# A decoder layer on one core: the low parts of every second weight chunk in three quarters of the MLP by an accumulating DMA

## The chip, the cores and the metric

The kernel runs on one core of one Trainium2 chip. The metric is the time of the whole program on the device, in microseconds, the median over runs. A profiled execution gives, beside that, a trace of every engine: TensorE (PE, its weight loads PEld), VectorE (DVE), ScalarE (ACT), GpSimd (POOL), SyncE (SP, which issues the loads) and the 16 DMA engines.

## What is computed

One layer of a hybrid decoder for 256 tokens of width 2048: three token mixers on one input projection (sliding-window attention, gated delta rule, cross-attention over memory tokens), a gated merge, an output projection, an MLP of width 8192, and a last norm, all with fp32 weights.

```python
n = rms_norm(h, g_mix[l])
p = n @ w_in[l]
...
merged = g_a * (y_a @ w_swa_up[l]) + g_b * (y_b @ w_gdn_up[l]) + g_c * (y_c @ w_xa_up[l])
h = h + merged @ w_out[l]
u = rms_norm(h, g_mlp[l]) @ w_mlp_in[l]
h = h + jnp.square(jax.nn.relu(u)) @ w_mlp_out[l]
...
return rms_norm(h, g_final)
```

The change is in the last three quarters of the two MLP products.

## The kernel before

**Products in high and low parts.** Every weight and activation is held as the sum of two numbers of type `float32r`: a high part (the fp32 value rounded) and a low part (what rounding left). A product is made of high by high, high by low and low by high.

**The weight stream.** All weights come as a stream of 496 chunks, in the order of use. A chunk is 128 partitions by 1024 fp32, 512 KB: two blocks of 128 rows of the weights by 512 columns. A chunk is loaded from SP's queue into a buffer `raw` (`issue_dma`; 4 buffers, `RAW`), ACT copies it into `whi`, which rounds it, and DVE makes `wlo = raw - whi` (`split`, L234 to L237; 4 buffers each, `SPL`). `weights` (L143) is called by a strip for each chunk. It first issues loads up to AHEAD + RAW - 1 = 5 chunks ahead and splits up to AHEAD = 2 chunks ahead, in program order. A buffer is free for its next chunk when the last reader of the chunk before is done: for `raw` that is DVE's subtraction, for `whi` and `wlo` the last matmul.

**Strips.** `strip_w` (L157) computes 512 output columns with the weights as the stationary operand: per chunk 8 pairs of matmuls, L168 with 512 moving columns (high and low activations at once) and L169 with 256. `strip_x` (L182, through `mm_x`) keeps activations stationary and moves weights: per chunk 12 matmuls of 512 columns, three for each of two blocks of rows and two halves of the tokens (L178 to L180). Both kinds of strip have 8 chunks.

**The MLP** (L160 on) goes by quarters of the hidden width: in each, 4 strips of the first kind make the hidden values, and 4 of the second kind add their part to the output. The hidden values are moved out of PSUM by a chain over the engines (`hid_evac`): ACT copies a half (L230), DVE adds (L232) and scales (L1173), POOL squares (L1175), ACT rounds and DVE subtracts (L235, L237 on `ys`). Between the first and the second quarter (`q == 1`) the space of the merged mixers' tile `mg` is given up, and the gain of the last norm, `gf`, is loaded there. Chunks 304 to 495 belong to the last three quarters.

**Order.** Every engine takes its instructions in the order in which the program was written; generators (`start`, `advance`, `run`) lay the steps of a split or of a chain a hop at a time beside the products.

Of the kernel before, what the change touches and what calls it, by code (L numbers as in the profile page):

```python
# [10 lines left out]
F32 = mybir.dt.float32  # L11
# [12 lines left out]
CW = 1024  # columns per partition of a chunk of streamed weights  # L24
# [3 lines left out]
TAIL = 3         # last chunks that stay on chip together  # L28
# columns in which the output is scaled and stored: whether by the scalar engine, which
FIN = (0, slice(0, 256)), (1, slice(1536, 2048)), (0, slice(256, 1536))  # L30
# The background work is a row of steps, taken at a rate per tick (a block of products of the main stream), so
# that what a step reads has been made by then: rates of attention and decays, of the delta rule, of the
# convolution, of the sliding window.
RATE_A, RATE_B, RATE_C, RATE_S = 0.53, 0.5, 0.6, 0.83
# ticks between a sum in PSUM and what follows it, in the output projection; before its norm
OUT, WO = 8, 3
# chunks at which x's squares, its scaling and the norm of the memory tokens begin
XSQ, XSC, MRS = 4, 13, 13
NEG = -1.0e30
RAW, SPL = 4, 4  # chunks loaded, chunks split into high and low parts  # L40
AHEAD = 2        # chunks split ahead of the one in the products

# columns of the packed vectors
V_GMIX, V_GMEM, V_GMLP, V_CONV, V_NORM, V_SINK, V_ALOG, V_DTB, V_END = (
    0, 16, 32, 48, 96, 97, 113, 117, 121)
# blocks of the packed constants
C_ID, C_PREV, C_CUR, C_CUM, C_BLK, C_DEC, C_DECN, C_BS, C_PLACE, C_LVL = range(10)
BS = 16          # block of the lower matrices inverted by substitution
# [5 lines left out]
def tile_layer(ctx: ExitStack, tc: tile.TileContext, xT, memT, wmk, wmv, wq, wkv, wqc, wqkv, wz, wg, wua, wub, wuc, wo, w1, w2, vec, cst, x, gfin, out):  # L54
# [7 lines left out]
    wspl = pool("wspl", SPL)  # L62
# [60 lines left out]
    def pieces(i, w):  # L123
        """The first chunk comes in a block of rows at a time."""
        n = KC if i == 0 else 1
        return [slice(w // n * k, w // n * (k + 1)) for k in range(n)]

    def issue_split(i):
        raw = raws.pop(i)
        w = raw.shape[-1]  # L130
        hi = wspl.tile([P, WMAX], F32R, name="whi")[:, :w]
        lo = wspl.tile([P, WMAX], F32R, name="wlo")[:, :w]
        parts[i] = hi, lo
        fs = before_split[i]
        if i:
            for f in fs:
                f()
        for n, c in enumerate(pieces(i, w)):
            if i == 0:
                fs[n]()  # L140
            start(split(hi[:, c], lo[:, c], raw[:, c]))

    def weights(ncols):  # L143
        """High and low parts of the next chunk of the stream; loads and splits run ahead."""
        i = done[2]
        while done[0] < min(len(stream), i + AHEAD + RAW):
            issue_dma(done[0])
            done[0] += 1
        while done[1] < min(len(stream), i + AHEAD + 1):
# [7 lines left out]
    def strip_w(k0, nk, acts, evac, nblk=4):  # L157
        """out.T = W.T @ acts for 512 columns of W: 128 of them at a time in one PSUM bank, whose
        halves hold the products with the high and with the low parts of acts."""
# [15 lines left out]
    def mm_x(bank, acts, k, tt, hi, lo, first, last):  # L175
        """out (tokens on partitions) += acts.T @ W for one block of 128 rows of W."""
# [5 lines left out]
    def strip_x(acts, evac):  # L182
        """out = acts.T @ W for 512 columns of W, tokens on partitions."""
# [11 lines left out]
    def last_strip_x(acts, evac):  # L195
        """The same in halves of the columns. The last chunks stay on chip together, and the halves of the
        tokens and columns are finished one after the other."""
# [17 lines left out]
    # What engines do to a finished bank, or in the background, is a generator that yields where one  # L215
    # engine hands over to another; tick() moves all of them on by a hop.
# [21 lines left out]

    def split_scaled(hi, lo, src, g):
# [9 lines left out]
    def rsqrt(out, in_, mul, n):  # L249
        """out = (in_ * mul + EPS) ** -0.5 on [P, n]"""  # L250
# [4 lines left out]
    def token_rstd(sums, rows, cols):  # L255
        """From sums of squares per partition and token: 1/rms as a row on each partition, and as a
        column with tokens on partitions."""
# [19 lines left out]
    class Lane:  # L277
        """Generators in a row, each with its rate in hops a tick; one may yield how many hops its last step
        counts for."""
# [39 lines left out]
    def pipelined(tasks, every):  # L319
        """Each task's hops one after the other, with those of the next task beginning `every` hops later."""  # L320
# [27 lines left out]
    # ================= start: memory tokens and x =================  # L348
# [94 lines left out]
    # ================= input projection =================  # L443
# [6 lines left out]
    # the keys of the sliding window, transposed: by kv head the high parts on all rows; the low parts on its rows  # L450
    kp = sw.tile([P, 3, T], F32R, name="kp")
    head_rows = slice(0, 64), slice(64, 128)
    # v of the kv heads by block of keys: [high | low] of the first, [low | high] of the second
# [126 lines left out]
    def decays():  # L580
        dtb = vc_[:, V_DTB:V_DTB + 4].unsqueeze(1).broadcast_to([P, NT, 4])
        # softplus(t) = max(t, 0) + log1p(e), e = exp(-|t|); log1p(e) = ln(w) + (e - (w - 1)) / w, w = 1 + e
# [89 lines left out]
    def delta():  # L672
# [11 lines left out]
        # of a chunk, the columns for w and those for q: [w | q] in the first chunk, [q | w] in the second  # L684
# [591 lines left out]
```

## Time and profile before

| | us |
|---|---|
| median of 3 runs | 1503.67 |
| lowest and highest run | 1499.26, 1503.81 |
| span of the profiled execution, first to last instruction | 1498.2 |
| TensorE busy | 1466.9 (98%) |
| DVE busy | 956.9 (64%) |
| ACT busy | 748.5 (50%) |
| POOL busy | 189.7 (13%) |
| packets of the load queue, share of 16 engines | 54.0% |

The time of a run holds the span and what lies around it; the profiled execution has no time of its own beside the three runs, which are 1.1 to 5.6 us above its span. Busy is the time in which an engine worked on any instruction. Matmuls are pipelined and their ends are modelled, so a busy TensorE isn't one at its peak: how fast it goes is read from the starts of neighbouring matmuls. A mean over the span mixes stages, so what holds in the MLP is read from stretches of it.

### The profile page before, as it was taken

To read this page: it belongs to the slowest core of one execution; us is meant where nothing else is said; L and a number is where in the kernel's file an instruction comes from. 1 tells how busy PE (TensorE), PEld (TensorE's weight loads), DVE (VectorE), ACT (ScalarE), POOL (GpSimd) and SP (SyncE) were. 2 spreads that over 40 slices of the span, in tenths; PEclk is the share of its full clock that TensorE was granted. 3 is DMA by queue.
4 is the path that set the end of the run, shared out by engine and by line. 5 is a ranking of instruction groups with operands and counts; after the bars stand their busy time and mean duration, and the time that the engine had idled before them with its cause. 6 is when DMAs were issued, how large, how long until landed. Compare 5 with 4: busy or idle time off the path is not lost.

```text
span 1498.2 us, 20793 instructions
## 1 busy us (share of the span) xinstructions
PE 1466.9 (98%) x7890; PEld 1251.1 (84%) x7890; DVE 956.9 (64%) x1324; ACT 748.5 (50%) x1115; POOL 189.7 (13%) x244
## 2 busy tenths in 40 slices
PE   6999999998999999999999999999999999999997
PEld 5798888887888888888888888888888888888887
DVE  8866785774667786666557664476455665467554
ACT  5555754553465665454555443355334453345443
POOL 5200032143112210000001000011000010001011
PEclk9999999999999999999999999999999999999999
DMA  7555554444434555556655655655655655555653
GB/s 255 187 171 183 169 175 149 141 167 140 143 118 150 169 167 191 191 170 225 217 176 175 214 185 186 223 183 170 209 185 168 210 185 188 190 189 166 208 191 119
DMA packets 76069, 269.60 MB, mean 180 GB/s; under 512 B 8512, under 2 KB 9152, under 8 KB 75840
## 3 DMA queue, kind: packets, MB, share of 16 engines
q1 hardware_dynamic: 75968, 268.27, 54.0%
q8 instruction: 62, 1.02, 0.3%
q14 instruction: 39, 0.32, 0.1%
HBM read 266.14 MB, written 2.10 MB: 179 GB/s over the span
## 4 chain that ended last, share of the span: by engine, by line
PE 74%; ACT 1%; DVE 1%; issue 0%; DVEq 0%; POOLq 0%; POOL 0%; ACTq 0%
PE mm L168 28%; PE mm L169 14%; PE mm L180 10%; PE mm L179 10%; PE mm L178 10%; PE mm L337 1%; PE mm L954 1%; PE mm L953 0%; ACT whi L235 0%; DVE wlo L237 0%; ACT L975 0%; ACT L1051 0%; PE mm L1006 0%; ACT sg L1051 0%; PE mm L1005 0%
## 5 line engine op out<-in xcount | busy, mean ns | idle before, releaser
L237 DVE TENSOR_TENSOR wlo<-raw,whi 128x1024 fp32r<-128x1024 f32 (+2 forms) x497 | 613.5, 1249 | 349.1 <-ACT whi L235 348.4
L168 PE MATMUL mm<-xs,whi 128*128 128x512 f32 x2240 | 796.6, 397 | 0.4 <-DVE half L232 0.4
L235 ACT CAST whi<-raw 128x1024 fp32r<-128x1024 f32 (+2 forms) x497 | 511.5, 1041 | 434.2 <-PE mm L180 209.1
L169 PE MATMUL mm<-xs,wlo 128*128 128x256 f32 x2240 | 627.5, 280 | 1.1 <-DVE wlo L237 1.1
L168 PEld LDWEIGHTS mm<-xs,whi 128*128 128x128 f32 x2240 | 421.0, 188 | 99.6 <-issue 0.9
L169 PEld LDWEIGHTS mm<-xs,wlo 128*128 128x128 f32 x2240 | 421.4, 188 | 2.6 <-DVE wlo L237 2.0
L180 PE MATMUL mm<-whi,ys 128*128 128x512 f32 (+1 forms) x544 | 209.6, 385 | 0.0
L179 PE MATMUL mm<-wlo,ys 128*128 128x512 f32 (+1 forms) x544 | 207.4, 381 | 0.0
L178 PE MATMUL mm<-whi,ys 128*128 128x512 f32 (+1 forms) x544 | 206.3, 379 | 0.0
L230 ACT COPY half<-mm 128x256 f32<-128x256 f32 x192 | 70.5, 373 | 141.7 <-PE mm L169 140.2
L179 PEld LDWEIGHTS mm<-wlo,ys 128*128 128x128 f32 x544 | 102.1, 188 | 23.3
L178 PEld LDWEIGHTS mm<-whi,ys 128*128 128x128 f32 x544 | 102.1, 188 | 21.5
L180 PEld LDWEIGHTS mm<-whi,ys 128*128 128x128 f32 x544 | 102.3, 188 | 20.7
L1175 POOL TENSOR_TENSOR half<-half 128x256 f32<-128x256 f32 x64 | 40.0, 626 | 577.9 <-DVE half L1173 571.5
L168 PE MATMUL mm<-ys,whi 128*128 128x512 f32 x256 | 91.2, 397 | 0.0
L232 DVE TENSOR_TENSOR half<-mm,half 128x256 f32<-128x256 f32 x120 | 49.2, 418 | 43.7 <-ACT half L230 43.4
L169 PE MATMUL mm<-ys,wlo 128*128 128x256 f32 x256 | 71.8, 280 | 0.0
L1106 DVE TENSOR_TENSOR res<-mm,res 128x512 f32<-128x512 f32 (+1 forms) x42 | 28.0, 666 | 52.3 <-PE mm L180 52.3
L168 PEld LDWEIGHTS mm<-ys,whi 128*128 128x128 f32 x256 | 48.1, 188 | 10.7 <-issue 0.2
L178 PE MATMUL mm<-whi,mg 128*128 128x512 f32 x128 | 50.5, 394 | 0.0
L180 PE MATMUL mm<-whi,mg 128*128 128x512 f32 x128 | 49.9, 390 | 0.0
L179 PE MATMUL mm<-wlo,mg 128*128 128x512 f32 x128 | 49.9, 390 | 0.0
(259 smaller groups left out, 1128.8 us busy)
## 6 DMA issues: line engine op xcount, KB each, us to landing
raw<-in_w SPq DMA_DIRECT2D x256, 512.0 KB, 4.2
raw<-in_wg SPq DMA_DIRECT2D x96, 512.0 KB, 3.3
raw<-in_wo SPq DMA_DIRECT2D x32, 512.0 KB, 4.4
raw<-in_wqkv SPq DMA_DIRECT2D x24, 512.0 KB, 4.0
raw<-in_wq SPq DMA_DIRECT2D x16, 512.0 KB, 3.9
raw<-in_wua SPq DMA_DIRECT2D x16, 512.0 KB, 4.8
raw<-in_wmv SPq DMA_DIRECT2D x8, 512.0 KB, 3.8
raw<-in_wqc SPq DMA_DIRECT2D x8, 512.0 KB, 3.9
```

Source lines behind the costliest of these rows:

```text
L168: nc.tensor.matmul(banks[b], lhsT=hi[:, i, cols], rhs=acts[:, k], start=(k == k0), stop=False)
L169: nc.tensor.matmul(banks[b][:, :T], lhsT=lo[:, i, cols], rhs=acts[:, k, 0], start=False, stop=(last and i == KC - 1))
L178: nc.tensor.matmul(bank, lhsT=acts[:, k, 0, tok], rhs=hi, start=first, stop=False)
L179: nc.tensor.matmul(bank, lhsT=acts[:, k, 0, tok], rhs=lo, start=False, stop=False)
L180: nc.tensor.matmul(bank, lhsT=acts[:, k, 1, tok], rhs=hi, start=False, stop=last)
L230: nc.scalar.copy(out=t, in_=bank[:, T:])
L232: nc.vector.tensor_tensor(out=out, in0=bank[:, :T], in1=t, op=ALU.add)
L235: nc.scalar.copy(out=hi, in_=src)
L237: nc.vector.tensor_tensor(out=lo, in0=src, in1=hi.bitcast(F32), op=ALU.subtract)
L337: nc.tensor.transpose(ps[:, i * P:(i + 1) * P], src_fn(i), ident)
L1106: nc.vector.tensor_tensor(out=v, in0=bank, in1=v, op=ALU.add)
L1175: nc.gpsimd.tensor_tensor(out=t, in0=t, in1=t, op=ALU.mult)
```

## The change

From the second quarter of the MLP on, new chunks are split into a second pool with 6 buffers each of `whi` and `wlo`, which lies where `mg` was, and loads and splits run two chunks further ahead (`AHEAD_2` = 4). Of these chunks those with an odd number are split in another way: ACT copies `raw` into `whi` as before, makes `wlo = -whi` in a second pass, and a DMA issued from POOL then adds `raw` to `wlo` in place. All three are issued at once, without hops between them. Even chunks are split as before. Comments that the change also takes out are left out here.

```diff
-RAW, SPL = 4, 4  # chunks loaded, chunks split into high and low parts
-AHEAD = 2        # chunks split ahead of the one in the products
...
+RAW, SPL = 4, 4
+AHEAD = 2
+AHEAD_2, SPL_2 = 4, 6
...
-    wspl = pool("wspl", SPL)
+    spl = [pool("wspl", SPL)]
...
-        hi = wspl.tile([P, WMAX], F32R, name="whi")[:, :w]
-        lo = wspl.tile([P, WMAX], F32R, name="wlo")[:, :w]
+        late = len(spl) > 1
+        hi = spl[-1].tile([P, WMAX], F32R, name="whi")[:, :w]
+        lo = spl[-1].tile([P, WMAX], F32R, name="wlo")[:, :w]
         parts[i] = hi, lo
+        if late and i % 2:
+            start(split_dma(hi, lo, raw))
+            return
...
-        while done[0] < min(len(stream), i + AHEAD + RAW):
+        ahead = AHEAD if len(spl) == 1 else AHEAD_2
+        while done[0] < min(len(stream), i + ahead + RAW):
             issue_dma(done[0])
             done[0] += 1
-        while done[1] < min(len(stream), i + AHEAD + 1):
+        while done[1] < min(len(stream), i + ahead + 1):
...
+    def split_dma(hi, lo, src):
+
+        nc.scalar.copy(out=hi, in_=src)
+        nc.scalar.activation(out=lo, in_=hi.bitcast(F32), func=AF.Copy, scale=-1.0)
+        nc.gpsimd.dma_start(out=lo, in_=src, accum_op=ALU.add)
+        yield
...
+            spl.append(ctx.enter_context(tc.tile_pool(name="wspl2", bufs=SPL_2)))
```

On ACT, at the end of the first strip of the second quarter, before (L230 copies a sum out of PSUM, `ys` are hidden values, `whi` the copies of chunks; the semaphores that a row waits for stand in brackets, DMAHW for a load, DMASW for a DMA of POOL):

```order
L235 CAST whi<-raw 128x1024 [waits DMAHW7_49,DVE_49,PE_49]
L230 COPY half<-mm 128x256 [waits PE_49] x3
L230 COPY half<-mm 128x256 [waits DVE_49,PE_49]
L235 CAST ys<-half 128x256 [waits Pool_49]
L235 CAST whi<-raw 128x1024 [waits DMAHW0_49]
L235 CAST ys<-half 128x256 [waits Pool_49] x3
L235 CAST whi<-raw 128x1024 [waits DMAHW1_49]
```

And now, at the same place:

```order
L241 CAST whi<-raw 128x1024 [waits DMAHW0_49,DVE_49,PE_49]
L247 CAST whi<-raw 128x1024 [waits DMAHW1_49,PE_49]
L248 ACTIVATE wlo<-whi 128x1024 [waits DMASW1_49,PE_49,Activation_49]
L236 COPY half<-mm 128x256 [waits PE_49] x3
L236 COPY half<-mm 128x256 [waits DVE_49,PE_49]
L241 CAST ys<-half 128x256 [waits Pool_49]
L241 CAST whi<-raw 128x1024 [waits DMAHW2_49]
L241 CAST ys<-half 128x256 [waits Pool_49] x3
L247 CAST whi<-raw 128x1024 [waits DMAHW3_49]
L248 ACTIVATE wlo<-whi 128x1024 [waits DMASW2_49,Activation_49]
```

Ahead of the sums two more chunks have been split, every second chunk takes two passes on ACT, and the second of them waits for the accumulate that filled the same buffer six chunks before.

On SP, the loads of the same strip, before:

```order
L121 DMA raw<-in_w 128x1024 [waits DMAHW3_49,DVE_49]
L121 DMA raw<-in_w 128x1024 [waits DMAHW4_49,DVE_49]
L121 DMA raw<-in_w 128x1024 [waits DMAHW5_49,DVE_49]
L121 DMA raw<-in_w 128x1024 [waits DMAHW6_49,DMAHW2_49,DVE_49]
L121 DMA raw<-in_w 128x1024 [waits DMAHW7_49,DVE_49]
```

And now:

```order
L122 DMA raw<-in_w 128x1024 [waits DMAHW3_49,DMASW1_49]
L122 DMA raw<-in_w 128x1024 [waits DMAHW6_49,DVE_49]
L122 DMA raw<-in_w 128x1024 [waits DMAHW5_49,DMAHW2_49,DMASW2_49]
L122 DMA raw<-in_w 128x1024 [waits DMAHW0_49,DVE_49]
L122 DMA raw<-in_w 128x1024 [waits DMAHW7_49,DMASW3_49]
L122 DMA raw<-in_w 128x1024 [waits DMAHW1_49,DMASW4_49,Activation_49]
L122 DMA raw<-in_w 128x1024 [waits DMAHW2_49,DVE_49]
```

Each load waited for a subtraction on DVE; now, but for one place in eight chunks, every second one waits for an accumulate. TensorE's matmuls stand in the same order as before.

## Rows read from the trace of the kernel before

**Rows 1.** The page: busy us, share of the span, instructions.

```profile
PE 1466.9 (98%) x7890; PEld 1251.1 (84%) x7890; DVE 956.9 (64%) x1324; ACT 748.5 (50%) x1115; POOL 189.7 (13%) x244
```

**Rows 2.** Stretches of the MLP: strips of the first kind, then of the second.

```profile
core 0: us, PE busy (x) PEld busy (x) DVE busy (x) ACT busy (x) POOL busy (x), PEclk, DMA share, GB/s
950.00:1040.00 90.00, 90.00 (x513) 78.29 (x512) 56.21 (x70) 41.17 (x57) 7.50 (x12) 1.00 0.58 194
1040.00:1130.00 90.00, 90.00 (x390) 72.54 (x389) 48.11 (x50) 36.91 (x41) 2.50 (x4) 1.00 0.58 188
```

**Rows 3.** TensorE by line, 940 to 1480: busy us, mean ns, idle us before.

```profile
L168 PE MATMUL mm<-xs,whi 128*128 128x512 f32 x768 | 269.1, 393 | 0.0
...
L178 PE MATMUL mm<-whi,ys 128*128 128x512 f32 (+1 forms) x405 | 154.9, 382 | 0.0
```

**Rows 4.** Waits, 950 to 1480: us in total, times, longest us.

```profile
POOL half L1175 <- DVE half L1173: 502.6, 36, 108.3
DVE wlo L237 <- ACT whi L235: 166.1, 117, 1.7
ACT whi L235 <- PE mm L180: 133.4, 77, 1.8
ACT whi L235 <- PE mm L168: 94.1, 54, 1.8
```

**Rows 5.** The load queue's waits, 950 to 1480.

```profile
SPq L121 <- DVE wlo L237: 360.8, 174, 6.8
```

**Rows 6.** Matmuls in order of time (start us, us), three places.

```profile
719.67 0.39 PE L178 MATMUL mm<-whi,mg 128*128 128x512 f32 x1
...
720.35 0.39 PE L178 MATMUL mm<-whi,mg 128*128 128x512 f32 x1
...
1085.05 0.39 PE L178 MATMUL mm<-whi,ys 128*128 128x512 f32 x1
...
1085.75 0.39 PE L178 MATMUL mm<-whi,ys 128*128 128x512 f32 x1
...
1139.68 0.39 PE L168 MATMUL mm<-xs,whi 128*128 128x512 f32 x1
...
1140.38 0.39 PE L168 MATMUL mm<-xs,whi 128*128 128x512 f32 x1
```

**Rows 7.** DVE by line, 950 to 1480.

```profile
L237 DVE TENSOR_TENSOR wlo<-raw,whi 128x1024 fp32r<-128x1024 f32 x189 | 233.5, 1252 | 166.1 <-ACT whi L235 166.1
```

**Rows 8.** Tile raw, 950 to 1480: ns min/median/max; landing of loads.

```profile
L235 ACT CAST whi<-raw x190: 1031/1048/1058, 949.4 to 1479.0; 128x1024 fp32r<-128x1024 f32 x190
...
L121 SPq DMA_DIRECT2D raw<-in_w x186: 327/328/328, 954.0 to 1472.6; - x186
...
DMA to landing us min/median/max: 3.1/4.2/7.4
```

**Rows 9.** ACT by line and shape, whole span.

```profile
L1051 ACT ACTIVATE sg<-sg 128x1024 f32<-128x1024 f32 x12 | 12.7, 1062 | 0.1
```

**Rows 10.** POOL by line, 950 to 1480.

```profile
L1193 POOL TENSOR_TENSOR res<-res,gf 128x512 f32<-128x512 f32 x6 | 7.8, 1299 | 59.1 <-ACT mm L1110 58.8
```

**Rows 11.** ACT in order of time at a strip's end.

```profile
1019.44 0.37 ACT L230 COPY half<-mm 128x256 f32<-128x256 f32 x1 [0.33 <-PE mm L169]
...
1022.59 0.41 ACT L235 CAST ys<-half 128x256 fp32r<-128x256 f32 x1 [0.68 <-POOL half L1175]
```

**Rows 12.** Stretches at the start, columns as in the second group.

```profile
8.00:12.00 4.00, 3.56 (x10) 2.74 (x11) 3.58 (x3) 3.44 (x7) 3.39 (x2) 1.00 1.01 355
12.00:16.00 4.00, 3.64 (x20) 2.91 (x19) 4.00 (x4) 3.49 (x7) 3.73 (x3) 1.00 1.03 392
16.00:20.00 4.00, 1.41 (x7) 1.05 (x6) 4.00 (x3) 3.65 (x6) 3.84 (x3) 0.92 0.36 139
20.00:24.00 4.00, 4.00 (x16) 3.12 (x14) 4.00 (x3) 0.30 (x1) 3.83 (x3) 0.66 0.91 300
...
32.00:36.00 4.00, 4.00 (x25) 3.55 (x24) 4.00 (x6) 1.05 (x1) 0.00 (x0) 1.00 1.00 381
```

## The prediction

> **What bounds the kernel now.** I read the page's table of busy time first, then a table of stretches for the MLP, then what each engine waits for there, and last the starts of single matmuls. The busy table [rows 1] puts TensorE at 98% of the span, DVE at 64%, ACT at 50%. A mean over stages can mislead, so the stretch table [rows 2] cuts out the part that the change touches, from 950 us on: TensorE is busy 90.00 of 90.00 us in strips of both kinds, at a granted clock of 1.00 (the 2.4 GHz level), while DVE has 56 or 48 us of work, ACT 41 or 37, POOL 7.5 or 2.5 and the DMA engines a share of 0.58. The groups of TensorE in this part [rows 3] show idle time 0.0 in front of all five lines of matmuls (the first and the last of them stand there): nothing that DVE, ACT or a transfer does is late there. The waits [rows 4] run the other way: ACT's copy of a chunk waits for a matmul (the buffer is free only when TensorE is done with it), DVE waits for that copy, and the load queue waits for DVE's subtraction [rows 5]. Feeders wait for TensorE, not TensorE for feeders.
>
> The time of a chunk comes from starts [rows 6]: in a strip with tokens on the output, three matmuls take 1085.05 to 1085.75, 0.70 us, and a chunk has twelve: 2.80 us. In a strip of the first kind, two pairs take 1139.68 to 1140.38, 0.70 us, and a chunk has eight pairs: 2.80 us again. The three quarters have 192 chunks, 538 us. The first two of them are split before the new buffers exist, so of the odd ones 95 are changed.
>
> **What is removed.** 95 subtractions of 1.25 us [rows 7] leave DVE: 119 us of work, all of it in a stretch where TensorE never waited for DVE. Worth nothing on the path: with DVE faster, TensorE is still the next late thing. A chunk's low part was made in time before, and earlier is no use.
>
> **What is added on ACT.** One more pass over 128x1024 per changed chunk. The copy of that shape takes 1.05 us [rows 8], an activation of that shape 1.06 [rows 9], so 95 x 1.06 = 101 us. In 90 us stand 32 chunks, 16 changed, 17 us more on 41 [rows 2]: 58 of 90. ACT stays under two thirds, and its own waits for matmuls (133 + 94 us, [rows 4]) shrink by that much. Cost nothing, covered by those waits.
>
> **What is added on POOL.** 95 issues. POOL sits idle 503 us there for DVE's input to its squares [rows 4]. An issue waits for ACT's second pass, and behind it in POOL's queue stand the squares of a strip's end; but ACT does that pass ahead of the copies that feed those squares (order of ACT above), so the squares are not held longer than the issue itself takes. I bound an issue between the 0.33 us that the load queue spends on one [rows 8] and the 1.3 us of POOL's longest operation there [rows 10], and take 1; it lies beside TensorE's work.
>
> **Is a low part ready in time?** Before, a chunk was split two ahead; now a set of buffers comes back six chunks later, so ACT may begin a chunk when TensorE begins the one five before it: a lead of 5 x 2.80 = 14.0 us. It has to hold 1.05 + 1.06 = 2.1 us on ACT and the accumulate, from the issue to its last byte. No row shows an accumulate. Its nearest row is a load of the same 512 KB, 3.1 us at least, 4.2 in the median, 7.4 at most [rows 8]. Below lies 3.1 (no dearer than a load), above twice the median plus the issue, 9.4; I take 4.2 and a second pass over the bytes, 1.4 (next part): 5.6. Then 2.1 + 5.6 = 7.7 of 14.0, and 6.3 us are over; even 9.4 fits. At the end of a strip of the first kind ACT first moves out the sums: from the last copy at 1019.44 to the last cast at 1022.59 + 0.41 it is held 3.6 us [rows 11]. The next odd chunk then has 10.4 us for its 7.7.
>
> **Do the raw buffers come back in time?** This is the added wait: the load queue, one row for all loads, now waits in every second row for an accumulate instead of a subtraction (order of SP above), and every later load stands behind it. The slot that an accumulated chunk leaves goes to the chunk five later (one time in four: four later), a subtracted chunk's to the third or fourth after it. Over eight chunks a slot passes one of each: 2.1 + 5.6 + a load of 4.2, and 1.05 + 1.25 + 4.2, together 18.4 of the 22.4 us that eight chunks last. The one return after four chunks (11.9 us against 11.2) is 0.7 late, and the 6.3 us of lead cover it. TensorE waits only if accumulate plus two loads exceed 18 us (now 14.0). Cost nothing; without that cover it would be 24 times the excess.
>
> **Do the DMA engines keep up?** This is the term that decides. In three stretches at the start they are all busy (share 1.00 to 1.03) and move 381 and 392 GB/s, once 355 [rows 12]. At 386, 524,288 bytes take 1.36 us of all engines. Two chunks last 5.60 us; their loads need 2.72, so an accumulate may cost **2.88 us** before the transfers bound. Below: one pass, 1.36 (then 4.08 of 5.60). Above: three passes in turn, raw read, low part read, low part written, 4.08 (then 6.80). I take two passes, 2.72, since in a load reading and writing already run side by side and count once, and the add has one read more. That is 5.44 of 5.60, 97%: the transfers fit, with almost no room. The Trainium skill ("Collectives: The Full Stack", The bandwidth ceiling) says of adds in the transfer path that two source reads slow them, not the add; by it the cost is two passes and the sum stays 0, and no run here shows it.
>
> **Sum.** 0 on DVE, ACT, POOL, lead, slots and DMA engines. The last chunk is odd too, but its low part is due 7.7 us after a start 14.0 us ahead, and TensorE's end is as before. So the profiled execution would again span 1498.2 us. The runs lie 1.1 to 5.6 us above that span, their median 5.5; forecast at the median, **1503.7**.
>
> **Rivals.** First, *slower: the DMA engines become the bound.* The place is the load queue in the last three quarters, the point 2.88 us per accumulate. Beyond it each pair of chunks lasts longer by the excess: 95 x (cost - 2.88), less the 6 us of lead. At 3.2 us: 30 - 6 = +24, 1528. At 4.08: 114 - 6 = +108, 1612. Against it: only a third pass or a transfer slower than a load reaches it. For it: 97% leaves 0.16 us, and a single slow engine of sixteen holds up the whole transfer. A fall of the granted clock is not added: it fell to 0.66 after a stretch in which TensorE was busy 1.41 of 4.00 us [rows 12], and here it would be busy over 80%. The Trainium skill ("DMA: Bandwidth & Descriptors", Latency and other measured facts) says that engines 7 and 15 are usually slower, by a guess because of transfers issued from POOL; no trace here has such a transfer, and 3% would be enough.
>
> Second, *slower: the raw buffers come back late,* if accumulate plus two loads exceed 18 us, say 9 + 2 x 5 = 19: 24 times 1.0, less 6: +18, 1522. Loads of 7.4 us occur [rows 8], but as the longest of 186.
>
> Third, *faster: a shorter matmul pitch.* Three matmuls on the tile `mg` take 719.67 to 720.35, 0.68 us [rows 6], against 0.70 on `ys`, though shapes and moving buffers are the same. So operands, by place or by value, can move the pitch by 3%. The new buffers lie where `mg` lay. If the 96 chunks of the second kind of strip took 4 x 0.68 = 2.72 us, that is 96 x 0.08 = -7.7, 1496. Against it: no row tells place from value, and `ys` and its values stay. It might as well go up by as much, 1511.
>
> That the change does nothing is not a rival but the forecast: DVE's 119 us go, and the time does not.
>
> **How the numbers follow.** About 0.3% (4.5 us) is what a measurement of this kernel can tell from no change. Forecast, within it: 0.54. DMA engines: of costs between 1.36 and 4.08, those beyond 2.88 + (6 + 4.5)/95 = 2.99 are 40%; I give 0.30, since two passes are the likeliest. Late slots 0.06. Pitch: 0.08 down, 0.02 up. So faster 0.08, same 0.54, slower 0.38. The range goes from 1495 (pitch gain) to 1558, an accumulate of (54 + 6)/95 + 2.88 = 3.5 us; that leaves out about half of the DMA case and little else.
>
> **What would show it.** Right: subtractions of this size on DVE down by 95, DVE near 840 us, ACT near 850, TensorE's idle time in the last three quarters still 0.0, a DMA share up to 0.97 or less, accumulates landing 4 to 8 us after issue. The DMA rival: share near 1.0 there, TensorE waiting for an accumulate or ACT's copy waiting for a load. The slot rival: the same waits at a share well below 1. Pitch: three matmuls off 0.70 us without idle time. The forecast is wrong if an accumulate costs more than 2.99 us of the sixteen engines or needs more than 10 us to land.

## The result, and the profile after

The changed kernel takes 1547.33 us (median of 4, 1545.97 to 1551.86) where the kernel before takes 1501.56 on the same chip: a ratio of 1.0308, 95% interval 1.0291 to 1.0324. It is 46 us slower. The time lies in the range given, but the forecast was no change; the direction was wrong. The profiled execution spans 1544.2 us against 1498.2, so 46.0 us are to be found in it.

Busy time over the whole span, columns as in [rows 1]:

```profile
PE 1478.2 (96%) x7890; PEld 1250.7 (81%) x7890; DVE 844.6 (55%) x1229; ACT 844.4 (55%) x1210; POOL 271.6 (18%) x339
```

DVE fell by 112 us and ACT rose by 96, as intended, and it bought nothing. The same two stretches as in [rows 2]:

```profile
950.00:1040.00 90.00, 85.38 (x479) 73.30 (x478) 37.14 (x54) 52.50 (x68) 20.77 (x27) 1.00 0.96 259
1040.00:1130.00 90.00, 85.14 (x370) 67.25 (x369) 26.62 (x33) 48.91 (x53) 15.53 (x19) 1.00 0.96 257
```

TensorE, full before, is busy 85 of 90 us in both kinds of strip, at the same granted clock of 1.00; it has 479 matmuls in the first stretch where [rows 2] has 513. The DMA engines' share went from 0.58 to 0.96. TensorE by line, 940 to 1480 us, answering to [rows 3] (L174 and L175 are the strips of the first kind, L184 to L186 those of the second):

```profile
L174 PE MATMUL mm<-xs,whi 128*128 128x512 f32 x768 | 271.2, 395 | 0.0
L175 PE MATMUL mm<-xs,wlo 128*128 128x256 f32 x768 | 216.6, 282 | 15.9 <-DMA wlo<-raw 15.6
L185 PE MATMUL mm<-wlo,ys 128*128 128x512 f32 x332 | 133.5, 402 | 12.7 <-DMA wlo<-raw 12.6
L184 PE MATMUL mm<-whi,ys 128*128 128x512 f32 x333 | 131.3, 394 | 0.0
```

The two lines that read low parts now wait, nearly always for the accumulating DMA; over the whole span the page has 17.0 and 19.4 us for them, and the rest of the 46 stands in TensorE's busy time (1478.2 against 1466.9), probably because a matmul that is held within a group is drawn longer. That names who waits last, not why. The waits of the feeders, 950 to 1480, answer to [rows 4], and those of the load queue to [rows 5]:

```profile
ACT whi L247 <- DMA raw<-in_w: 124.3, 62, 7.7
...
ACT whi L241 <- DMA raw<-in_w: 74.6, 46, 3.5
...
ACT whi L241 <- PE mm L186: 2.6, 1, 2.6
```
```profile
SPq L122 <- DMA wlo<-raw: 297.4, 84, 8.0
SPq L122 <- DVE wlo L243: 108.4, 50, 4.7
```

Before, ACT's copies waited for TensorE (133 and 94 us). Now that wait is all but gone and they wait 199 us for loads, and the load queue waits 297 us for accumulates. The direction has turned: TensorE waits for feeders that no longer wait for TensorE. The transfers themselves, from issue to landing, 950 to 1530 (queue, packets, MB, share of 16 engines; then count, size, median us):

```profile
q1 hardware_dynamic: 26969, 98.26, 48.0%
q0 software_dynamic: 13680, 49.81, 46.4%
...
raw<-in_w SPq DMA_DIRECT2D x186, 512.0 KB, 5.5
wlo<-raw POOLq DMA_DIRECT2D x95, 512.0 KB, 6.6
```

An accumulate costs 0.464 x 580 / 95 = 2.83 us of all sixteen engines, a load 0.480 x 580 / 186 = 1.50. Last, the chain of work that ended last (start us, us, what), two laps of it:

```profile
1290.54 8.49 DMA wlo<-raw
...
1299.08 4.76 DMA raw<-in_w
...
1303.92 1.06 ACT whi L247
...
1305.97 1.04 ACT whi L241
...
1307.03 1.24 DVE wlo L243
...
1308.28 4.24 DMA raw<-in_w
...
1312.59 3.11 issue
...
1315.71 5.50 DMA wlo<-raw
...
1321.68 8.87 DMA raw<-in_w
...
1330.65 1.06 ACT whi L241
...
1331.74 1.24 DVE wlo L243
...
1332.99 4.68 DMA raw<-in_w
...
1337.73 2.44 issue
...
1340.19 7.12 DMA wlo<-raw
```

There is no TensorE in these two laps (over 950 to 1530 us the transfers make 59% of the chain, and TensorE's lines less than 20%). An accumulate lands, the load that waited for its raw buffer starts, ACT copies, DVE subtracts, the next load starts into the buffer so freed, ACT copies and negates ("issue" here, up to POOL's start), and the next accumulate begins. POOL's issues in that stretch tell how far a lap goes (start us, us; in brackets the idle time before):

```profile
1290.54 0.87 POOL L249 DMA_DIRECT2D wlo<-raw  x1 [5.60 <-ACT wlo L248]
1296.42 0.87 POOL L249 DMA_DIRECT2D wlo<-raw  x1 [5.01 <-ACT wlo L248]
1306.36 0.87 POOL L249 DMA_DIRECT2D wlo<-raw  x1 [9.07 <-ACT wlo L248]
1309.34 0.87 POOL L249 DMA_DIRECT2D wlo<-raw  x1 [2.11 <-ACT wlo L248]
1315.71 0.89 POOL L249 DMA_DIRECT2D wlo<-raw  x1 [5.50 <-ACT wlo L248]
```

From 1290.54 to 1315.71 are four accumulates, eight chunks, in 25.17 us; the next lap, to 1340.19, takes 24.48. TensorE needs 22.4. This is the way of a raw buffer which the prediction worked out at 18.4 us. Over the whole part (ns min/median/max, first and last start):

```profile
L249 POOL DMA_DIRECT2D wlo<-raw x95: 860/869/1075, 950.1 to 1523.9; - x95
```

These 95 accumulates begin 6.10 us after each other, 24.4 per eight chunks, 2.0 too many; times 24 laps that is 48 us, for a loss of 46.

### The profile page after: what moved, and what is told of

The parts are those of the page before. It is cut to its first block, busy times and chain, and to the rows that moved or that the text cites. A ratio compares the mean times of both kernels' runs of the same rounds, so it can differ in the third digit from the quotient of the medians.

```text
span 1544.2 us, 21028 instructions
## 1 busy us (share of the span) xinstructions
PE 1478.2 (96%) x7890; PEld 1250.7 (81%) x7890; DVE 844.6 (55%) x1229; ACT 844.4 (55%) x1210; POOL 271.6 (18%) x339
## 4 chain that ended last, share of the span: by engine, by line
PE 44%; DMA 22%; ACT 4%; issue 3%; DVE 3%; POOL 0%; SPq 0%; POOLq 0%; DVEq 0%; ACTq 0%
PE mm L174 19%; DMA wlo<-raw 12%; DMA raw<-in_w 10%; PE mm L175 10%; PE mm L185 4%; PE mm L184 4%; PE mm L186 4%; ACT whi L247 1%; ACT whi L241 1%; DVE wlo L243 1%; ACT wlo L248 1%; DVE half L1187 1%; DVE half L238 1%; PE mm L350 1%; PE mm L967 1%
## 5 line engine op out<-in xcount | busy, mean ns | idle before, releaser
L174 PE MATMUL mm<-xs,whi 128*128 128x512 f32 x2240 | 798.5, 397 | 0.4 <-DVE half L238 0.4
L243 DVE TENSOR_TENSOR wlo<-raw,whi 128x1024 fp32r<-128x1024 f32 (+2 forms) x402 | 501.1, 1257 | 517.4 <-ACT whi L241 516.5
L175 PE MATMUL mm<-xs,wlo 128*128 128x256 f32 x2240 | 628.6, 281 | 17.0 <-DMA wlo<-raw 15.6
L241 ACT CAST whi<-raw 128x1024 fp32r<-128x1024 f32 (+2 forms) x402 | 412.9, 1037 | 289.0 <-DMA raw<-in_w 83.1
L174 PEld LDWEIGHTS mm<-xs,whi 128*128 128x128 f32 x2240 | 421.5, 188 | 99.4 <-issue 0.9
L175 PEld LDWEIGHTS mm<-xs,wlo 128*128 128x128 f32 x2240 | 421.7, 188 | 23.0 <-DMA wlo<-raw 20.3
L185 PE MATMUL mm<-wlo,ys 128*128 128x512 f32 (+1 forms) x544 | 210.2, 386 | 19.4 <-DMA wlo<-raw 19.2
L184 PE MATMUL mm<-whi,ys 128*128 128x512 f32 (+1 forms) x544 | 207.9, 382 | 0.0
L186 PE MATMUL mm<-whi,ys 128*128 128x512 f32 (+1 forms) x544 | 207.1, 381 | 0.0
L249 POOL DMA_DIRECT2D wlo<-raw x95 | 82.9, 872 | 522.8 <-ACT wlo L248 373.8
L247 ACT CAST whi<-raw 128x1024 fp32r<-128x1024 f32 x95 | 99.8, 1050 | 136.5 <-DMA raw<-in_w 135.2
L184 PEld LDWEIGHTS mm<-whi,ys 128*128 128x128 f32 x544 | 102.1, 188 | 22.2
L186 PEld LDWEIGHTS mm<-whi,ys 128*128 128x128 f32 x544 | 102.3, 188 | 21.1
L248 ACT ACTIVATE wlo<-whi 128x1024 fp32r<-128x1024 f32 x95 | 100.7, 1060 | 3.0
L174 PE MATMUL mm<-ys,whi 128*128 128x512 f32 x256 | 91.2, 397 | 0.0
L175 PE MATMUL mm<-ys,wlo 128*128 128x256 f32 x256 | 71.7, 280 | 0.0
L174 PEld LDWEIGHTS mm<-ys,whi 128*128 128x128 f32 x256 | 48.1, 188 | 10.8 <-issue 0.2
L1075 POOL TENSOR_TENSOR half<-half,sg 128x256 f32<-128x256 f32 x32 | 26.0, 830 | 162.9 <-DVE half L238 162.9
```

The lines of the kernel that those rows point to most:

```text
L174: nc.tensor.matmul(banks[b], lhsT=hi[:, i, cols], rhs=acts[:, k], start=(k == k0), stop=False)
L175: nc.tensor.matmul(banks[b][:, :T], lhsT=lo[:, i, cols], rhs=acts[:, k, 0], start=False, stop=(last and i == KC - 1))
L184: nc.tensor.matmul(bank, lhsT=acts[:, k, 0, tok], rhs=hi, start=first, stop=False)
L185: nc.tensor.matmul(bank, lhsT=acts[:, k, 0, tok], rhs=lo, start=False, stop=False)
L186: nc.tensor.matmul(bank, lhsT=acts[:, k, 1, tok], rhs=hi, start=False, stop=last)
L241: nc.scalar.copy(out=hi, in_=src)
```

## The experiments

Two theories stood at the start. **DMA engines:** 0.96 is as good as full, and the accumulates take more than the engines have. **Raw buffers:** a buffer is held until its accumulate has landed, the loads behind it in the one queue come late, and the rest follows. After the first four kernels a third came up, that the low parts are simply late for TensorE by the time that the accumulate takes (**late low parts**). All diffs are against the changed kernel unless said; ratios are to the kernel before on the same chip.

| kernel | us, median | ratio, 95% interval |
|---|---|---|
| changed | 1547.3 | 1.0308, 1.0291 to 1.0324 |
| ahead_only | 1500.4 | 0.9999, 0.9990 to 1.0007 |
| traffic | 1501.0 | 1.0006, 0.9994 to 1.0019 |
| copy_only | 1503.2 | 1.0022, 1.0013 to 1.0031 |
| raw8 | 1517.2 | 1.0115, 1.0099 to 1.0132 |
| hold_raw | 1513.2 | 1.0082, 1.0062 to 1.0101 |
| late_low | 1506.4 | 1.0042, 1.0027 to 1.0058 |
| deep | 1509.5 | 1.0056, 1.0039 to 1.0072 |
| every4 | 1500.5 | 0.9998, 0.9989 to 1.0008 |
| hold_act | 1543.0 | 1.0269, 1.0225 to 1.0313 |
| raw5 | 1528.4 | 1.0191, 1.0154 to 1.0227 |
| neg_dve | 1554.5 | 1.0355, 1.0333 to 1.0376 |
| lead20 | 1553.0 | 1.0349, 1.0316 to 1.0381 |

**ahead_only**: the new buffers and the longer lead, without accumulates.

```
-        if late and i % 2:
-            start(split_dma(hi, lo, raw))
-            return
```

> The new pool of 6 buffers and the longer lead, but every chunk is split by DVE as before; no accumulating DMA. Theory 1 (the DMA engines have too little room for the accumulates): as before, 1501 us, DMA share 0.58 in the last three quarters. Theory 2 (raw buffers come back too late after an accumulate): as before, 1501. Rival that the place of the new buffers changes the pitch of the matmuls: 1494 or 1509.

Measured 1500.4. The pool, its place in memory and the lead cost nothing and gain nothing; the loss is the accumulates'.

**traffic**: low parts from DVE as before, and beside them 92 accumulating DMAs of the same size (the changed kernel has 95), from the high part into four scratch tiles.

```
+            start(split_busy(hi, lo, raw, aside[i // 2 % 4]))
...
+    def split_busy(hi, lo, src, to):
+        nc.scalar.copy(out=hi, in_=src)
+        nc.gpsimd.dma_start(out=to, in_=hi.bitcast(F32), accum_op=ALU.add)
+        yield
+        nc.vector.tensor_tensor(out=lo, in0=src, in1=hi.bitcast(F32), op=ALU.subtract)
```

> As ahead_only, and beside it 92 accumulating DMAs of the same size from POOL, one for every second chunk, which add the high part into four tiles that nobody reads: the DMA engines get the same work, but no load and no product waits for an accumulate, and raw buffers come back after DVE's subtraction. The result is the reference's. Theory 1 (throughput of the DMA engines): two chunks need about 5.9 us or more of the engines as in the changed kernel, 1535 to 1548 us, share over 0.95, ACT waiting for loads. Theory 2 (raw buffers late): nothing is held, 1501 to 1506 us.

Measured 1501.0, the time of before. Its two stretches, columns as in [rows 2], and its transfers from 950 to 1480:

```profile
950.00:1040.00 90.00, 90.00 (x514) 78.39 (x513) 60.22 (x75) 40.14 (x56) 19.05 (x25) 1.00 0.92 262
1040.00:1130.00 90.00, 90.00 (x390) 72.48 (x389) 49.63 (x53) 37.88 (x42) 17.32 (x21) 1.00 1.03 297
...
raw<-in_w SPq DMA_DIRECT2D x186, 512.0 KB, 7.7
wlo<-whi POOLq DMA_DIRECT2D x92, 512.0 KB, 8.2
```

The engines carry all of these bytes at TensorE's pace, at a share of 0.92 to 1.03, and in the median transfers are slower than in the changed kernel (7.7 and 8.2 us to land, against 5.5 and 6.6) without TensorE losing anything. The theory of the DMA engines falls: what matters is not how busy they are, but who waits for a transfer.

**copy_only**: a plain copy in place of the add.

```
-        nc.gpsimd.dma_start(out=lo, in_=src, accum_op=ALU.add)
+        nc.gpsimd.dma_start(out=lo, in_=src)
```

> The changed kernel with a plain copy in place of the adding one: the DMA from POOL writes raw into the low part. Left out is the addition, so low parts are the whole weight. Theory 1: one pass in place of two, about 160 ns for a packet of 4 KB in place of 328, 4.1 us of the engines for two chunks of 5.6: 1501 to 1505 us, share about 0.8. If it is POOL's issue or its order that costs, not the bytes: 1540 or more, as with the addition.

Measured 1503.2, +0.2%. Same waits, same buffers, as many issues (0.54 us of POOL each instead of 0.87); the transfer lands in 5.2 us instead of 6.6, the loads in 4.8 instead of 5.5. The load queue still waits 281 us for these DMAs, and TensorE 0.6 us. So the structure of waits alone costs some 3 us; it is the duration that the waits hold which decides, and 1.4 us less in one transfer and 0.7 in the others take nearly all of the loss away.

**raw8**: four more raw buffers (in tiles which the old pool leaves idle) and loads four chunks further ahead.

```
+        more = i >= 324 and i % 8 >= 4
+        raws[i] = (spl[0].tile([P, WMAX], F32, name="whi") if more else wraw.tile([P, WMAX], F32, name="raw"))[:, :w]
...
-        while done[0] < min(len(stream), i + ahead + RAW):
+        while done[0] < min(len(stream), i + ahead + (8 if i >= 316 else RAW)):
```

> The changed kernel with 8 raw buffers in place of 4 from chunk 324 on (the old pool's idle high-part buffers are the other four), loads running 4 chunks further ahead. Theory 1 (throughput): the share stays at or above 0.96, only the longer stock helps, 4 chunks or some 11 us: 1533 to 1547 us. Theory 2 (raw buffers late): loads no longer wait for accumulates, 1501 to 1508 us at a share near 1.0.

Measured 1517.2: 30 of the 46 us are back. The rest is not raw buffers, or not these alone: ACT's copies wait for TensorE again, but the accumulates now land in 8.8 to 9.2 us, and TensorE still waits 11 us for them.

**hold_raw**: as traffic, but the DMA adds the raw chunk, so that it holds the raw buffer. Against traffic:

```
-        nc.gpsimd.dma_start(out=to, in_=hi.bitcast(F32), accum_op=ALU.add)
+        nc.gpsimd.dma_start(out=to, in_=src, accum_op=ALU.add)
```

> As traffic (every odd chunk's low part comes from DVE, an accumulating DMA of 512 KB runs beside it into scratch tiles that nobody reads), with one word changed: the DMA adds the raw chunk in place of its high part, so the raw buffer is held until the transfer has landed, as in the changed kernel. TensorE never waits for the transfer itself. Theory that the raw buffers come back late: the load queue waits for the accumulates again, the loads come late, ACT's copy waits for them, and most of the loss is back although no product needs what the DMA writes: near 1530 us (1522 to 1545). Rival, that the low parts themselves come late: traffic's time, 1501 (1499 to 1504), TensorE busy 90.00 of 90.

Measured 1513.2, between the two. Holding the buffer costs 12 us where the same bytes from another tile cost none; but it is far from 46.

**late_low**: the reverse; the raw buffer is free after ACT's copy, and only the products wait for the DMA.

```
-        nc.gpsimd.dma_start(out=lo, in_=src, accum_op=ALU.add)
+        nc.gpsimd.dma_start(out=lo, in_=hi.bitcast(F32), accum_op=ALU.add)
```

> The changed kernel, but the DMA adds the high part instead of the raw chunk to the negated high part, so the raw buffer is free after ACT's copy and only the products wait for the transfer. The low part of these chunks is left out by this (it becomes zero). Theory that the raw buffers come back late: the larger part of the loss goes, as with eight raw buffers, 1501 to 1517 us, the load queue no longer waits for accumulates, and what is left is low parts that land late at the ends of strips. Rival, that the low parts come late in the first place: 1535 to 1550, TensorE still waits some 35 us for accumulates.

Measured 1506.4. The transfers from 950 to 1480, and TensorE's line of the first kind of strip that reads low parts, 940 to 1480:

```profile
wlo<-whi POOLq DMA_DIRECT2D x95, 512.0 KB, 8.4
```
```profile
L175 PE MATMUL mm<-xs,wlo 128*128 128x256 f32 x768 | 215.2, 280 | 0.9 <-DMA wlo<-whi 0.6
```

Here the accumulates land in 8.4 us, later than in the changed kernel, and TensorE waits for them less than 1 us. So a lead of 14.0 us holds an accumulate that takes longer than the one it was said to be too short for. In the chain of this kernel from 950 to 1530 us, transfers into `wlo` make 9%, against 31.5% in the changed one. But 12 us (hold_raw) and 5 us (late_low) do not make 46, so each half alone leaves something out. What hold_raw leaves out of the raw buffer's way is ACT's negation.

**deep**: eight raw buffers, and eight pairs of split buffers with a split six chunks ahead.

```
+        more = i >= 318 and i % 8 >= 6
+        hi = (spl[0].tile([P, WMAX], F32R, name="wlo") if more else spl[-1].tile([P, WMAX], F32R, name="whi"))[:, :w]
+        lo = (spl[0] if more else spl[-1]).tile([P, WMAX], F32R, name="wlo")[:, :w]
...
+        ahead = AHEAD if len(spl) == 1 else AHEAD_2 + 2 * (i >= 316)
```

(with the lines of raw8; removed lines are left out)

> The changed kernel with eight raw buffers and eight pairs of split buffers from chunk 316 to 324 on (in the tiles that the old pool leaves idle), and a split six chunks ahead instead of four: lead 19.6 us instead of 14.0. Theory that the loss is all latency (30 us raw buffers, 16 us low parts that come late): both covered, 1501 to 1507 us, TensorE busy 89 to 90 of 90, DMA share near 1.0. Rival, that the DMA engines are short by a little when the adds feed the products: still 1515 or more, with the DMA share at 1.0 and TensorE waiting for accumulates all along.

Measured 1509.5, and the stretches show where:

```profile
950.00:1040.00 90.00, 85.20 (x476) 73.07 (x475) 38.26 (x55) 56.87 (x73) 20.75 (x27) 1.00 0.97 284
1040.00:1130.00 90.00, 90.00 (x402) 73.04 (x401) 30.15 (x35) 55.47 (x59) 17.27 (x21) 1.00 1.05 305
1130.00:1220.00 90.00, 90.00 (x503) 77.90 (x502) 37.30 (x54) 58.20 (x73) 21.43 (x28) 1.00 0.97 273
1220.00:1310.00 90.00, 90.00 (x400) 73.06 (x399) 28.94 (x34) 52.91 (x56) 16.52 (x21) 1.00 1.03 289
```

Most of the loss lies in the first stretch, in which the buffers are taken into use; from 1040 to 1490 us TensorE is busy throughout and the chain is TensorE's alone, with every accumulate of the change in place and feeding the products, at a share of 0.97 to 1.05 in the stretches shown. So the DMA engines were not what was short, but the buffers that hold the time of the transfers.

**every4**: an accumulate for every fourth chunk.

```
-        if late and i % 2:
+        if late and i % 4 == 1:
```

> The changed kernel with every fourth chunk by an accumulating DMA instead of every second, four raw buffers as before. Two accumulates in eight chunks instead of four: DMA share near 0.8, accumulates land in 5 to 6 us, loads in 4.5. Latency theory: a raw slot is held by an accumulate half as often, the other slots come back early: 1500 to 1506 us. If the time went with the number of accumulates alone, half of the loss: 1524.

Measured 1500.5, the time of before, at a share of 0.77 (950 to 1480), loads landing in 4.3 us and accumulates in 5.0. Half of the accumulates cost nothing at all; the loss does not go with their number.

**hold_act**: hold_raw with ACT's negation put back, into the scratch tile. Against hold_raw:

```
         nc.scalar.copy(out=hi, in_=src)
+        nc.scalar.activation(out=to, in_=hi.bitcast(F32), func=AF.Copy, scale=-1.0)
         nc.gpsimd.dma_start(out=to, in_=src, accum_op=ALU.add)
```

> As hold_raw (accumulates of the raw chunk into scratch tiles that nobody reads, low parts from DVE, so no product needs a transfer's result), with the negating pass on ACT put back, into the scratch tile. The way of a raw buffer is then that of the changed kernel step by step: load, copy, negation, accumulate, load, copy, subtraction, load. Theory of the lap (eight chunks need 24.5 to 25.2 us on this way where TensorE needs 22.4, in the changed kernel as read from its trace; TensorE only follows): the loss is back although no product waits for an accumulate, 1535 to 1550 us, four accumulates per 24 us or more. Rival, that half of the loss is low parts that come late: hold_raw's 1513 and little more, up to 1522.

Measured 1543.0: the loss is back, though no product needs what any DMA writes. TensorE by line, 940 to 1480, and POOL's issues with first and last start:

```profile
L179 PE MATMUL mm<-xs,wlo 128*128 128x256 f32 x768 | 216.6, 282 | 10.6 <-DVE wlo L247 8.7 <-DVE wlo L256 1.9
L189 PE MATMUL mm<-wlo,ys 128*128 128x512 f32 x343 | 137.6, 401 | 6.7 <-DVE wlo L247 4.3 <-DVE wlo L256 2.3
```
```profile
L254 POOL DMA_DIRECT2D wlo<-raw x92: 860/869/1075, 969.7 to 1525.8; - x92
```

TensorE waits for DVE's subtractions now, which are late because the copies are, which are late because the loads are (ACT's copies wait 184 us for loads, 950 to 1480, and the load queue waits 302 us for accumulates). The pace is (1525.8 - 969.7) / 91 = 6.11 us for an accumulate, 24.4 per eight chunks, that of the changed kernel. In hold_raw and in traffic the same row reads

```profile
L253 POOL DMA_DIRECT2D wlo<-raw x92: 860/870/1127, 966.0 to 1491.1; - x92
```
```profile
L253 POOL DMA_DIRECT2D wlo<-whi x92: 862/872/1077, 965.0 to 1475.2; - x92
```

that is 23.1 and 22.4 us per eight chunks. One pass of 1.06 us on ACT, off TensorE's path and with ACT busy 55% of the span, costs 30 us, because it stands in a loop whose length is at the limit: 1.4 us more (4 x 6.11 against 4 x 5.77) for each of 23 laps. It is not ACT's work as such: late_low has the same pass on ACT, holds no raw buffer for an accumulate, and loses 5 us.

**raw5**: one more raw buffer.

```
+        if i >= 324 and i % 5 == 4:
+            if not fifth:
+                fifth.append(spl[0].tile([P, WMAX], F32, name="whi"))
+            raws[i] = fifth[0][:, :w]
...
-        while done[0] < min(len(stream), i + ahead + RAW):
+        while done[0] < min(len(stream), i + ahead + RAW + (i >= 316)):
```

> The changed kernel with a fifth raw buffer from chunk 324 on, loads one further ahead. Theory of the lap: a buffer passes one chunk of each kind in ten chunks instead of eight, 28.0 us at TensorE's pace against the 25 it needs, so one buffer takes away nearly all that four more did: 1505 to 1520 us, four accumulates per 22.4 to 23 us. Rival, that the loss lies in the sum of transfer times (DMA engines or low parts late): 1535 or more.

Measured 1528.4. One buffer takes away 19 of the 46 us, about two thirds of what four do, but I had expected 27 at least. Loads land in 6.2 us and accumulates in 7.4 (950 to 1480, in the four old buffers), longer than with four buffers alone: part of what the buffer gives, the longer transfers take. With the 5.4 to 7.7 us that the two laps above have beside their transfers, that makes a way of 25.2 to 27.5 us for ten chunks, which have 28.0, so a remainder is open: TensorE waits 19.3 us for accumulates here, spread over all stretches (87 of 90 busy in each up to 1400), and the chain runs through ACT's and DVE's work at the ends of strips.

**neg_dve**: the negation on DVE.

```
-        nc.scalar.activation(out=lo, in_=hi.bitcast(F32), func=AF.Copy, scale=-1.0)
+        nc.vector.tensor_scalar(out=lo, in0=hi.bitcast(F32), scalar1=-1.0, scalar2=None, op0=ALU.mult)
```

> The changed kernel with the negation on DVE instead of ACT (95 x 1.06 us off ACT). No transfer and no buffer changes. Theory of the lap: where the copy of the even chunk stands right behind the odd chunk's copy and negation on ACT, the lap loses that 1.06 us, in some of the 24 laps: 1520 to 1545 us. If ACT's order has no part in it: 1547.

Measured 1554.5, 7 us slower than the changed kernel, where either view had it no slower. DVE negates in 0.69 us instead of ACT's 1.06, but it works in order too: at strip ends its negation stands behind the sums, their scaling and the low parts of the hidden values. The chain there (start us, us, what):

```profile
1197.37 0.44 DVE half L238
...
1201.81 0.98 DVE wlo L243
...
1203.29 1.08 DVE ys L243 x3
1204.37 0.61 DVE wlo L248
...
1205.51 5.60 DMA wlo<-raw
```

Its accumulates begin between 956.6 and 1529.5 us, 6.09 us each, the pace of the changed kernel. So the extra 7 us go with the start and not with the laps: the first accumulate begins 6.5 us later than in the changed kernel (956.6 against 950.1), because its negation stands on DVE behind two sums of the strip before. Whether neg_dve loses at the strip ends just what it gains elsewhere, or the order on ACT costs nothing, this run does not tell.

**lead20**: half of deep; eight pairs of split buffers and a lead of 19.6 us, but four raw buffers.

> The changed kernel with eight pairs of split buffers in place of six and a split six chunks ahead instead of four (lead 19.6 us instead of 14.0), four raw buffers as before: half of deep. Theory of the lap (the way of a raw buffer, eight chunks of it in 24.5 us, does not pass TensorE): a longer lead can't be filled, since the loads come no earlier; nothing is won but the 5.6 us of a longer store at the start: 1540 to 1550 us. Rival, that low parts come late for want of lead: 1503 to 1520.

Measured 1553.0, not better than the changed kernel. It may be a little worse: its accumulates land in 7.0 us instead of 6.6 and begin 6.21 us after each other instead of 6.10, for which I have no shown cause. TensorE by line, 940 to 1480:

```profile
L176 PE MATMUL mm<-xs,wlo 128*128 128x256 f32 x768 | 217.9, 284 | 26.6 <-DMA wlo<-raw 26.6
...
L186 PE MATMUL mm<-wlo,ys 128*128 128x512 f32 x315 | 126.0, 400 | 11.5 <-DMA wlo<-raw 11.5
```

This view names the accumulate as what TensorE waits for, 38 us of it, and yet a lead longer by 5.6 us gains nothing. The theory of late low parts falls as the cause of the 46; hold_act shows that the way of the raw buffer is enough for it. Late low parts come second: with raw buffers in plenty (raw8) 17 us are still lost, 11 of them waits for accumulates, and the longer lead on top (deep) brings that to 8, most of it before 1040 us.

## Why the prediction was wrong, point by point

**What bounds the kernel, what is removed, what is added on ACT and POOL**: right. DVE at 844.6 and ACT at 844.4 us, where 840 and 850 were said; POOL's issue takes 0.87 us (1 was taken); none of it shows in TensorE's time when the DMA is not in the raw buffer's way (traffic). One sentence needs a correction: ACT's pass "cost nothing, covered by those waits". The waits were there, but the pass stood in a loop, and in the loop it costs (hold_act against hold_raw: 30 us).

**Do the DMA engines keep up?** Right, and narrowly so. Two passes were taken, 2.72 us of all engines; 2.83 was measured. They keep up: traffic and, from 1040 us on, deep run at TensorE's pace at a share near 1.0. The bound of 2.88 was not a sharp one, though. In the changed kernel two loads and an accumulate take 2 x 1.50 + 2.83 = 5.83 us of the engines, more than the 5.60 that two chunks last; in traffic the same three take 2 x 1.42 + 2.78 = 5.61 (from 49.7% and 48.2% of 530 us for 186 loads and 92 accumulates), with TensorE full. The busy time of a transfer is not a fixed price. The first rival, with a chance of 0.30 the one that carried the slower side, would have given the measured time at 3.4 us an accumulate, by a mechanism that is not there.

**Is a low part ready in time?** The accumulate was put at 5.6 us and landed in 6.6; 2.1 + 6.6 still fits into 14.0. As a step by itself it holds (late_low: 8.4 us to land, and TensorE waits less than 1 us for them). But the 14.0 us count from the moment at which ACT may begin, and ACT could not begin, because the loads were late.

**Do the raw buffers come back in time?** This is the step that failed. It had the right loop and the right condition (accumulate plus two loads may not exceed 18 us), the right price (24 times the excess), and wrong sizes in it. Two laps of the chain of the changed kernel stand above. They have 8.49 + 4.76 + 4.24 = 17.5 and 5.50 + 8.87 + 4.68 = 19.1 us of transfers, where 14.0 was taken, and 25.17 - 17.5 = 7.7 and 24.48 - 19.1 = 5.4 of everything else, where 4.4 was taken. The first difference has a plain reason: the loads were given 4.2 us, their median at a share of 0.58 [rows 8], one paragraph before the share was forecast at 0.97. At 0.96 they take 5.5 in the median and the accumulates 6.6, and the chain does not go by medians: each of the two laps holds one transfer that took longer than that (8.49, 8.87). The second is hand-overs and the order on ACT, where an even chunk's copy can stand behind the odd one's copy and negation (1303.92, 1305.97 in the chain). Neither was in the sum. With the mean of the two laps, the step's own formula gives 24 x (24.8 - 22.4) - 6 = 52 us, with the mean over all accumulates (24.4) 42 us; the runs show 46.

The cover that the step named was wrong too: "the 6.3 us of lead cover it". A lead covers one delay once; a loop that is too long delays in every lap. lead20 shows it: more lead, no gain.

**The rivals.** The second, late raw buffers, is what happened, at 0.06. Its example (9 + 2 x 5 = 19 us, 1522) was near in the size of the transfers; with the fixed part at 4.4 it came out 25 us short. That the range up to 1558 holds the measured time is luck: its upper end was drawn for accumulates that cost the engines 3.5 us, and they did not. The third, another pitch by place or value, is refuted for the place: ahead_only has the same buffers and 0.9999.

**What would show it.** Four of the five signs of "right" came (DVE, ACT, share 0.96, accumulates at 4 to 8 us in the median, 10.3 at most) and the fifth did not (TensorE's idle time). The two numbers by which the forecast was to be wrong, 2.99 us of the engines or 10 us to land, were not reached (2.83 in the mean, 6.6 in the median): they tested the steps one by one, and what failed was a sum of three transfers. And the signs could not tell the rivals apart: late raw buffers were to show at a share "well below 1", but they show at 0.96. Only the experiment that keeps the share and removes the wait (traffic) could.

**The forecast's base.** A run is some 1.8 us longer than its own span (1546.02 against 1544.2 for the changed kernel), so a span of 1498.2 stands for a time of 1500.0 and not of 1503.7. This error is small beside the 46.

## What to carry to other kernels

When work moves from an engine to a DMA, follow the buffer and not only the result: write down the whole way until it is filled again, with every transfer at the duration it has under the load that the change itself makes, add the hand-overs and what stands ahead in each queue, and compare the sum with what the buffer's count allows. If that sum is near the limit, each microsecond anywhere in it, also on an engine that is half idle, is paid once a lap. Here a longer lead alone gained nothing, and one more buffer gained 19 us, four more 30. And a busy share near 1.0 beside a waiting engine does not show that the share is the cause: put the same bytes where nobody waits for them.

## What the runs showed of the hardware

In the changed kernel an accumulating DMA from one on-chip tile into another took 2.83 us of the sixteen engines for 512 KB, and a load of 512 KB 1.50; in copy_only the same transfer without the add took 0.269 x 530 / 95 = 1.50. So the add nearly doubles it (1.9 times), about as two passes would.

The time from issue to landing of a load hardly grew with the engines' share up to 0.77, and more above (950 to 1480 us): a median of 4.2 us at 0.57 (before), 4.3 at 0.77 (every4), 4.8 at 0.84 (copy_only), 5.0 and 5.5 at 0.96 (hold_raw, the changed kernel) and 7.7 at 0.98 (traffic). The last three have nearly the same share; perhaps they differ in how many transfers are under way at once, because in the changed kernel and hold_raw loads wait for buffers and fewer are issued early; no run tried that by itself.

TensorE's clock played next to no part: in the changed kernel the granted clock is 1.00 (the 2.4 GHz level) in five of the six stretches of 90 us from 950 to 1490, though TensorE paused for 4 to 6 us in each, and 0.98 in the other (1130 to 1220), by an estimate (0.02 x 90 us) 2 us of the 46.
